# A decoder trunk in float32r: the low parts of its weights by an adding transfer, three-deep rings, squares in two tiles

## The chip, the cores and the metric

One core of a Trainium2 chip runs the whole program in one launch. The metric is the device time of one execution in microseconds (us). Two runs of the kernel before took 2085.44 and 2081.3 us, median 2083.37.

## What is computed

Two layers over x of shape (512 positions, 1024 channels), float32. Each layer has a feed-forward, a mixer and a second feed-forward:

```python
for l in range(DEPTH):                                   # DEPTH = 2
    x = x + 0.5 * _swiglu(_rms_norm(x, norm_ffn1[l]), ffn1_w_gate[l], ffn1_w_up[l], ffn1_w_down[l])
    h = _rms_norm(x, norm_mix[l])
    proj = (h @ w_in[l]).astype(jnp.float32)
    p_rwkv = _token_shift(proj[..., :D_SHIFT], shift_mu[l])
    y_rwkv = _rwkv7_mixer(p_rwkv, ...)                   # 6 heads of 64, a recurrence over time
    y_attn = _attention_mixer(proj[..., ...], ...)       # 6 heads of 64, three dilated windows
    y_conv = _conv_mixer(proj[..., ...], ...)            # 256 channels, 31 taps
    mix = jnp.concatenate([y_rwkv, y_attn, y_conv], axis=-1).astype(x.dtype)
    x = x + mix @ w_out[l]
    x = x + 0.5 * _swiglu(_rms_norm(x, norm_ffn2[l]), ffn2_w_gate[l], ffn2_w_up[l], ffn2_w_down[l])
```

`_swiglu` is `(silu(x @ w_gate) * (x @ w_up)) @ w_down` with 2816 hidden channels. All weights are float32 and come from DRAM.

## The kernel before, in words

x lies transposed in SBUF, channels on the 128 partitions, eight tiles x[j] of 128x512. Every large product is made in float32r from two parts of each factor, a high part (the value cast to float32r) and a low part (the value minus the high part): `mm3` (L116 to L121) issues three matmuls, high by high, high by low, low by high, into one PSUM tile.

**A weight slot.** `slot` (L105 to L114) brings in one piece of weights of up to 128x1024. SP issues the load into a tile `raw` (ring of three), ACT casts it into `hi` (L112), and DVE subtracts, lo = raw - hi (L113). `hi` and `lo` have rings of RB buffers each. There are 368 slots. A slot of 1024 columns feeds 24 matmuls of 512 columns.

**Feed-forward** (`ffn`, L224). For each of 22 hidden tiles f a gate slot and an up slot are multiplied with the norm's xh and xl. `gated` (L213) then makes g and u from PSUM with the norm's factor R on DVE (L216, L218), silu on ACT (L217), the product s*u on POOL (L219), the high part ah on ACT (L124) and the low part al on DVE (L125). After that each of eight output tiles j takes three slots of the down weights (8, 8 and 6 tiles of 128, L267). DVE adds the result to x[j] (L271), and `norm_tile` (L167) prepares the next norm: xh on ACT (L172), xl on DVE (L173), the square on ACT into the tile "sq" (L180, the first one into acc, L177), the running sum acc on POOL (L181). `norm_sum` (L195) reduces acc on PE, POOL takes the power (L186), `norm_spread` (L203) spreads it, and ACT copies it into R (L208).

**Mixer** (`mixer`, L290). 14 slots of the input projection `win` are worked through by `columns`; the preparation of the recurrence for three head pairs (`first`, `scores`, `fourth` and others) is woven in: GG (L491) and AR (L476) on DVE, XM (L498, L514) and BF (L508) on POOL. The 31 taps of the convolution (L1001, DVE) have a low priority and fill DVE. Then come 12 slots of the attention projections (`att_cols`, 768 columns each) beside the chunks of the recurrence (s1 to s4; p3 makes Z, L637; Sf, L665, on POOL), then attention, convolution and the output projection (`out`, 22 slots of 256 to 640 columns per layer). The mixer ends with eight slots of 384 columns, nine matmuls each, and after each the update of x[j] (L717) and `norm_tile`.

**Order.** A scheduler puts the instructions of each engine into a fixed order; each engine then works through its own queue in that order and waits at its head. A buffer of a ring is written again only when all readers of its former content are done. SP's queue holds the loads of weights, and among them the stores and loads of x and small transfers of the mixer.

Of the kernel before, what the change touches and what calls it, by code (L numbers as in the profile page):

```python
# [9 lines left out]
F32 = mybir.dt.float32  # L10
F32R = mybir.dt.float32r
AF = mybir.ActivationFunctionType
ALU = mybir.AluOpType
PSUM = bass.MemoryType.PSUM

P = 128
D = 1024
T = 512
# [1 line left out]
F = 2816  # L20
FT = F // P
EPS = 1e-6
RB = 2
LOWP = 3000
CPAD = 40
XPAD = 56
# [55 lines left out]
class Kern:  # L82
    def __init__(self, ctx, tc, I, out):
        self.tc, self.nc, self.I, self.out = tc, tc.nc, I, out
        self.depth = 2
        self.uid = 0
        self.ahead = []
        self.cp = ctx.enter_context(tc.tile_pool(name="cp", bufs=1))
        self.ring = ctx.enter_context(tc.tile_pool(name="ring", bufs=3))
        self.xpool = ctx.enter_context(tc.tile_pool(name="xpool", bufs=1))  # L90
        self.nrm = ctx.enter_context(tc.tile_pool(name="nrm", bufs=1))
        self.dp = ctx.enter_context(tc.tile_pool(name="dp", bufs=1, space=bass.MemoryType.DRAM))
        self.ps = ctx.enter_context(tc.tile_pool(name="ps", bufs=1, space=PSUM))
# [11 lines left out]
    def slot(self, src, cols, nm="w"):  # L105

        nc = self.nc
        raw = self.ring.tile([P, 1024], F32, tag="raw", name=self.n("raw"))
        hi = self.ring.tile([P, 1024], F32R, tag="hi", name=self.n("hi"), bufs=RB)
        lo = self.ring.tile([P, 1024], F32R, tag="lo", name=self.n("lo"), bufs=RB)  # L110
        self.wdma = nc.sync.dma_start(out=raw[:, :cols], in_=src)
        nc.scalar.copy(hi[:, :cols], raw[:, :cols])  # L112
        nc.vector.tensor_tensor(lo[:, :cols], raw[:, :cols], hi[:, :cols].bitcast(F32), op=ALU.subtract)  # L113
        return hi, lo  # L114

    def mm3(self, out, whi, wlo, xhi, xlo, first, last):  # L116
# [50 lines left out]
    def norm_tile(self, j):  # L167

        nc = self.nc
        x = self.x[j]  # L170
        g = self.gains[:, self.nidx * KT + j : self.nidx * KT + j + 1]
        nc.scalar.activation(self.xh[j], x, AF.Copy, scale=g)  # L172
        nc.vector.scalar_tensor_tensor(  # L173
            self.xl[j], x, g, self.xh[j].bitcast(F32), op0=ALU.mult, op1=ALU.subtract
        )
        if j == 0:
            nc.scalar.activation(self.acc, x, AF.Square)  # L177
        else:
            sq = self.nrm.tile([P, T], F32, tag="sq", name=self.n("sq"))
            nc.scalar.activation(sq, x, AF.Square)  # L180
            nc.gpsimd.tensor_tensor(self.acc, self.acc, sq, op=ALU.add)  # L181

# [949 lines left out]
```

## Time and profile before

| what | value |
| --- | --- |
| median of two runs | 2083.37 us |
| the profiled execution's own time | 2081.86 us |
| its span | 2080.1 us |
| granted clock of PE, mean | 0.99 |
| feed-forward stages | about 31 to 397, 698 to 1059 and 1059 to 1427, 1726 to 2080 us |
| mixers | about 397 to 698 and 1427 to 1726 us |
| HBM read | 183.47 MB |

The stages are read from the places where the sum of a norm is reduced in the chain of waits (L199 at 390.5, 698.6, 1059.5, 1420.4 and 1726.0 us). A row of a group of instructions reads: line, engine, operation, output<-input with partitions x elements, the count, then the busy time in us, the mean ns of one, and the idle time of the engine just before them with what ended it. A row of a wait reads: who, for whom, us in total, times, the longest. A row of a stage reads: its bounds and length, busy time and count of each engine, the granted clock, the DMA engines' share, GB/s.

### The profile page before, as it was taken

The numbers are of one execution on the slowest core, as the hardware profiler recorded it, in microseconds if no ns is written. First come the engines' busy times: TensorE is split into PE (matmuls) and PEld (weight loads), VectorE is DVE, ScalarE is ACT, GpSimd is POOL, SyncE is SP. The second block draws the span as 40 slices with busy tenths as digits, with TensorE's granted clock in tenths as the row PEclk, the third lists the DMA queues.
The fourth block names the chain that finished last, engine by engine and source line by source line (L and its number), as shares of the span: only waits on it lengthen the run. The fifth ranks groups of instructions, "written<-read, shape, count | busy, mean of one in ns | idle before, by whom it ended". The sixth has DMA issues, their size and how long they took to land.

```text
span 2080.1 us, 25896 instructions
## 1 busy us (share of the span) xinstructions
PE 2031.8 (98%) x10406; PEld 1653.1 (79%) x10406; DVE 1121.5 (54%) x1565; ACT 740.0 (36%) x1136; POOL 330.4 (16%) x298
## 2 busy tenths in 40 slices
PE   7999999999899999999999999999899999999999
PEld 5888888777776888888888888887687678888887
DVE  4555432598866654552345544336997665454422
ACT  4323222463365433222223232225533653232221
POOL 3111001131420311110111111012223211110000
PEclk9999999999999999999999999999999999999999
DMA  4333333312321433333333233332222133333332
GB/s 142 98 94 99 99 109 107 105 59 61 84 62 59 126 94 101 95 96 92 103 92 101 92 101 96 114 116 84 57 87 77 50 93 101 95 99 101 99 109 76
DMA packets 81863, 193.79 MB, mean 93 GB/s; under 512 B 26640, under 2 KB 32272, under 8 KB 81744
## 3 DMA queue, kind: packets, MB, share of 16 engines
q1 hardware_dynamic: 81312, 191.79, 30.1%
q8 instruction: 81, 1.33, 0.3%
q10 hardware_dynamic: 432, 0.36, 0.1%
q14 instruction: 38, 0.31, 0.0%
HBM read 183.47 MB, written 8.65 MB: 92 GB/s over the span
## 4 chain that ended last, share of the span: by engine, by line
PE 86%; DVE 8%; POOL 2%; issue 2%; ACT 2%; DMA 0%; SPq 0%; POOLq 0%; ACTq 0%; DVEq 0%
PE psg L119 25%; PE psg L121 25%; PE psg L120 25%; DVE lo L113 2%; DVE cacc L1001 1%; PE psg L915 1%; DVE Ei L584 1%; PE psb L485 1%; DVE tm L578 1%; PE psc L950 1%; PE psg L867 1%; POOL ast L895 1%; PE psg L941 1%; POOL acc L181 1%; PE psg L869 1%
## 5 line engine op out<-in xcount | busy, mean ns | idle before, releaser
L112 ACT CAST hi<-raw 128x1024 fp32r<-128x1024 f32 (+3 forms) x368 | 350.7, 953 | 1001.3 <-PE psg L120 575.4
L113 DVE TENSOR_TENSOR lo<-raw,hi 128x1024 fp32r<-128x1024 f32 (+3 forms) x368 | 508.2, 1381 | 347.1 <-ACT hi L112 321.1
L119 PE MATMUL psg<-xh,hi 128*128 128x512 f32 x1632 | 644.3, 395 | 7.1 <-ACT xh L172 7.1
L121 PE MATMUL psg<-xh,lo 128*128 128x512 f32 x1632 | 643.2, 394 | 1.2 <-DVE lo L113 1.1
L120 PE MATMUL psg<-xl,hi 128*128 128x512 f32 x1632 | 643.0, 394 | 0.0
L119 PEld LDWEIGHTS psg<-xh,hi 128*128 128x128 f32 x1632 | 309.5, 190 | 74.2 <-ACT xh L172 7.1
L121 PEld LDWEIGHTS psg<-xh,lo 128*128 128x128 f32 x1632 | 309.2, 189 | 67.9 <-DVE lo L113 2.7
L120 PEld LDWEIGHTS psg<-xl,hi 128*128 128x128 f32 x1632 | 309.2, 189 | 66.7 <-issue 2.9
L120 PE MATMUL psg<-al,hi 128*128 128x512 f32 x704 | 274.2, 389 | 0.0
L119 PE MATMUL psg<-ah,hi 128*128 128x512 f32 x704 | 274.2, 389 | 0.0
L121 PE MATMUL psg<-ah,lo 128*128 128x512 f32 x704 | 274.2, 389 | 0.0
L219 POOL TENSOR_TENSOR s<-s,u 128x512 f32<-128x512 f32 x88 | 113.6, 1291 | 808.7 <-ACT hi L112 652.2
L218 DVE TENSOR_TENSOR u<-psg,R 128x512 f32<-128x512 f32 x88 | 60.8, 691 | 272.0 <-PE psg L121 272.0
L121 PEld LDWEIGHTS psg<-ah,lo 128*128 128x128 f32 x704 | 132.2, 188 | 27.6
L119 PEld LDWEIGHTS psg<-ah,hi 128*128 128x128 f32 x704 | 132.2, 188 | 27.4
L120 PEld LDWEIGHTS psg<-al,hi 128*128 128x128 f32 x704 | 132.2, 188 | 27.1
L216 DVE TENSOR_TENSOR g<-psg,R 128x512 f32<-128x512 f32 x88 | 60.8, 691 | 132.6 <-PE psg L121 130.1
L181 POOL TENSOR_TENSOR acc<-acc,sq 128x512 f32<-128x512 f32 x42 | 68.4, 1628 | 379.8 <-ACT sq L180 379.8
L1001 DVE SCALAR_TENSOR_TENSOR cacc<-z,par,cacc 128x482 f32<-128x482 f32 (+14 forms) x120 | 95.2, 793 | 1.8
L124 ACT CAST ah<-s 128x512 fp32r<-128x512 f32 x88 | 54.9, 624 | 113.1 <-POOL s L219 113.1
L867 PE MATMUL psg<-hi,xh 128*128 128x384 f32 x192 | 68.7, 358 | 2.5 <-ACT nat L892 2.5
L868 PE MATMUL psg<-lo,xh 128*128 128x384 f32 x192 | 65.1, 339 | 0.0
(208 smaller groups left out, 1800.7 us busy)
## 6 DMA issues: line engine op xcount, KB each, us to landing
raw<-in_wgu_dram SPq DMA_DIRECT2D x176, 512.0 KB, 3.5
raw<-in_wd_dram SPq DMA_DIRECT2D x64, 512.0 KB, 3.5
raw<-in_win_dram SPq DMA_DIRECT2D x28, 512.0 KB, 3.5
raw<-in_wd_dram SPq DMA_DIRECT2D x32, 384.0 KB, 3.1
raw<-in_watt_dram SPq DMA_DIRECT2D x24, 384.0 KB, 3.1
raw<-in_wout_dram SPq DMA_DIRECT2D x28, 192.0 KB, 2.3
xs<-x SPq DMA_DIRECT2D x16, 256.0 KB, 2.0
x<-xs SPq DMA_DIRECT2D x16, 256.0 KB, 3.0
```

The source lines that it names most:

```text
L112: nc.scalar.copy(hi[:, :cols], raw[:, :cols])
L113: nc.vector.tensor_tensor(lo[:, :cols], raw[:, :cols], hi[:, :cols].bitcast(F32), op=ALU.subtract)
L119: mm(out, lhsT=whi, rhs=xhi, start=first, stop=False)
L120: mm(out, lhsT=whi, rhs=xlo, start=False, stop=False)
L121: mm(out, lhsT=wlo, rhs=xhi, start=False, stop=last)
L181: nc.gpsimd.tensor_tensor(self.acc, self.acc, sq, op=ALU.add)
L216: nc.vector.tensor_tensor(t[0], p[0], self.R, op=ALU.mult)
L218: nc.vector.tensor_tensor(t[1], p[1], self.R, op=ALU.mult)
L219: nc.gpsimd.tensor_tensor(t[2], t[2], t[1], op=ALU.mult)
L867: mm(o, lhsT=self.xh[kk][:, t], rhs=hi[:, s], start=kk == 0, stop=False)
L868: mm(o, lhsT=self.xh[kk][:, t], rhs=lo[:, s], start=False, stop=False)
L1001: nc.vector.scalar_tensor_tensor(a[:, d:], z[:, 0 : T - d], pa("dww", u * CW + j), a[:, d:], op0=ALU.mult, op1=ALU.add)
```

## The change

Four things. RB, the depth of the rings `hi` and `lo`, becomes 3. The first four slots are made as before. In all others ACT writes minus hi into lo, and a transfer issued by POOL adds raw, from SBUF to SBUF, into lo. The square of `norm_tile` goes by turns into the tiles "sq" and "R".

```diff
-RB = 2
+RB = 3
...
+        self.begun = 0
...
         nc.scalar.copy(hi[:, :cols], raw[:, :cols])
-        nc.vector.tensor_tensor(lo[:, :cols], raw[:, :cols], hi[:, :cols].bitcast(F32), op=ALU.subtract)
+        if self.begun < 4:
+            self.begun += 1
+            nc.vector.tensor_tensor(lo[:, :cols], raw[:, :cols], hi[:, :cols].bitcast(F32), op=ALU.subtract)
+        else:
+            nc.scalar.activation(lo[:, :cols], hi[:, :cols].bitcast(F32), AF.Copy, scale=-1.0)
+            nc.gpsimd.dma_start(out=lo[:, :cols], in_=raw[:, :cols], accum_op=ALU.add)
         return hi, lo
...
         if j == 0:
             nc.scalar.activation(self.acc, x, AF.Square)
         else:
-            sq = self.nrm.tile([P, T], F32, tag="sq", name=self.n("sq"))
+            sq = self.nrm.tile([P, T], F32, tag=("sq", "R")[j % 2], name=self.n("sq"))
             nc.scalar.activation(sq, x, AF.Square)
             nc.gpsimd.tensor_tensor(self.acc, self.acc, sq, op=ALU.add)
```

The load of `raw` waited in SP's queue for DVE's subtraction of three slots earlier; now it waits for the adding transfer of three slots earlier. Names below carry the scheduler's numbers; lines after the change are up to six higher.

POOL's queue where the first feed-forward begins, before: the last sum, the power, then nothing but products.

```order
L181 TENSOR_TENSOR acc_136<-acc_136,sq_172 128x512
L186 TENSOR_TENSOR rnt<-rnt,mh 128x4
L219 TENSOR_TENSOR s_314<-s_314,u_313 128x512
L219 TENSOR_TENSOR s_325<-s_325,u_324 128x512
L219 TENSOR_TENSOR s_398<-s_398,u_397 128x512
```

The same place now:

```order
L187 TENSOR_TENSOR acc_136<-acc_136,sq_172 128x512
L192 TENSOR_TENSOR rnt<-rnt,mh 128x4
L119 DMA lo_336<-raw_334 128x1024
L119 DMA lo_368<-raw_366 128x1024
L225 TENSOR_TENSOR s_314<-s_314,u_313 128x512
L225 TENSOR_TENSOR s_325<-s_325,u_324 128x512
L119 DMA lo_411<-raw_409 128x1024
L119 DMA lo_443<-raw_441 128x1024
L225 TENSOR_TENSOR s_400<-s_400,u_399 128x512
```

Two transfers stand ahead of each product s*u from here to the end of the stage.

ACT's queue in the middle of the first gate and up stage, before: one cast of a weight between silu and the cast of ah.

```order
L112 CAST hi_627<-raw_626 128x1024
L217 ACTIVATE s_617<-g_615 128x512
L112 CAST hi_658<-raw_657 128x1024
L124 CAST ah_622<-s_617 128x512
L112 CAST hi_700<-raw_699 128x1024
```

The same stage now:

```order
L113 CAST hi_1010<-raw_1009 128x1024
L118 ACTIVATE lo_1011<-hi_1010 128x1024
L130 CAST ah_930<-s_925 128x512
L113 CAST hi_1042<-raw_1041 128x1024
L223 ACTIVATE s_1000<-g_998 128x512
L118 ACTIVATE lo_1043<-hi_1042 128x1024
L113 CAST hi_1085<-raw_1084 128x1024
L118 ACTIVATE lo_1086<-hi_1085 128x1024
```

Each cast of a weight is followed by the write of minus hi (L118), directly or after a silu.

POOL's queue in the first mixer, beside the attention projections, before (ast and nat belong to the norm of attention's heads, Sf to the recurrence):

```order
L895 TENSOR_TENSOR ast_3747<-ast_3747,mh 128x6
L897 TENSOR_TENSOR nat_3749<-nat_3749,ast_3747 128x384
L665 TENSOR_TENSOR Sf_3958<-SVU_2572,fd_2577 64x192 x2
L665 TENSOR_TENSOR Sf_4144<-SVU_2572,fd_2577 64x192 x2
L895 TENSOR_TENSOR ast_3747<-ast_3747,mh 128x6
```

The same place now:

```order
L901 TENSOR_TENSOR ast_3830<-ast_3830,mh 128x6
L903 TENSOR_TENSOR nat_3832<-nat_3832,ast_3830 128x384
L119 DMA lo_3999<-raw_3997 128x768
L671 TENSOR_TENSOR Sf_4044<-SVU_2636,fd_2641 64x192 x2
L119 DMA lo_4087<-raw_4085 128x768
L119 DMA lo_4178<-raw_4176 128x768
L671 TENSOR_TENSOR Sf_4232<-SVU_2636,fd_2641 64x192 x2
L901 TENSOR_TENSOR ast_3830<-ast_3830,mh 128x6
```

Transfers stand between the results that the recurrence and the attention take from POOL.

## The prediction

> **What bounds the kernel now.** I read the page's busy shares first, then a table by stage, then the waits of PE, then the DMA rows.
>
> ```profile
> PE 2031.8 (98%) x10406; PEld 1653.1 (79%) x10406; DVE 1121.5 (54%) x1565; ACT 740.0 (36%) x1136; POOL 330.4 (16%) x298
> 80.00:240.00 160.00, 160.00 (x707) 132.52 (x707) 81.03 (x74) 48.33 (x59) 18.97 (x15) 1.00 0.31 98
> 397.00:500.00 103.00, 94.73 (x448) 71.86 (x447) 92.53 (x134) 59.06 (x91) 27.38 (x24) 0.92 0.19 56
> 500.00:560.00 60.00, 58.31 (x492) 51.55 (x492) 55.63 (x117) 23.02 (x42) 20.19 (x17) 1.00 0.34 90
> 560.00:640.00 80.00, 74.58 (x727) 55.19 (x725) 54.05 (x152) 44.50 (x116) 19.21 (x28) 0.98 0.20 58
> 640.00:697.00 57.00, 56.44 (x302) 42.30 (x302) 37.35 (x71) 29.46 (x59) 10.77 (x11) 1.00 0.35 103
> 1427.00:1530.00 103.00, 94.74 (x458) 71.94 (x457) 94.35 (x140) 59.29 (x91) 27.42 (x24) 0.95 0.20 56
> ```
>
> The columns of a stage are its length, the busy time of PE, PEld, DVE, ACT and POOL, the granted clock, the DMA share and GB/s. In the feed-forward (first stage shown) PE never stops: 707 matmuls in 160 us, 0.226 us each, so a weight slot of 24 matmuls lasts 5.43 us. DVE is half idle there, and work taken from it buys nothing. Only in the mixer (the other rows) is DVE nearly full (92.5 of 103 us) while PE has holes: 8.3, 1.7, 5.4 and 0.6 us, 15.9 us in all. The clock lost there is worth 8.2 us in the first mixer (0.08 of 103) and 5.2 us in the second. Two mixers hold at most 32 + 13 = 45 us. What PE waits for in the first one:
>
> ```profile
> PE psb L644 <- DVE Z L637: 4.1, 2, 3.7
> PE psb L485 <- DVE GG L491: 3.5, 1, 3.5
> PE psb L530 <- DVE vv L402: 2.2, 1, 2.2
> PE psb L485 <- DVE AR L476: 1.6, 1, 1.6
> ```
>
> GG, vv and AR (7.3 us) are results queued on a full DVE; Z is a step of the serial chunk chain and stays.
>
> **The subtractions that leave.** Of 368 subtractions 364 go. The rows that price them and what takes their place:
>
> ```profile
> 397.00:500.00 103.00, 14.24 (x10) 0.92 0.19 56
> L112 ACT CAST hi<-raw 128x1024 fp32r<-128x1024 f32 x268 | 281.9, 1052 | 818.0 <-PE psg L120 510.2 <-issue 302.5 <-PE psg L121 2.8
> L119 PE MATMUL psg<-xh,hi 128*128 128x512 f32 x1632 | 644.3, 395 | 7.1 <-ACT xh L172 7.1
> q1 hardware_dynamic: 81312, 191.79, 30.1%
> raw<-in_wgu_dram SPq DMA_DIRECT2D x176, 512.0 KB, 3.5
> L219 POOL TENSOR_TENSOR s<-s,u 128x512 f32<-128x512 f32 x88 | 113.6, 1291 | 808.7 <-ACT hi L112 652.2 <-DVE u L218 131.6 <-ACT s L217 24.9
> L218 DVE TENSOR_TENSOR u<-psg,R 128x512 f32<-128x512 f32 x88 | 60.8, 691 | 272.0 <-PE psg L121 272.0
> L124 ACT CAST ah<-s 128x512 fp32r<-128x512 f32 x88 | 54.9, 624 | 113.1 <-POOL s L219 113.1
> ```
>
> The first row is that stage for the line of the subtraction alone: 14.2 of DVE's 92.5 us. DVE falls to 78.3 of 103 and the taps, of low priority, can move into the room. I take two thirds of the 7.3 us: 4.9 us, and of the lost clock the share that the holes shrink by, 4.9 / 8.3 = 0.59: 4.8 us in the first mixer, 3.1 in the second. That is -9.7 and -8.0, **-17.7 us**; bounds 0 and -45.
>
> **The new chain of a slot in the feed-forward.** When PE leaves a slot, ACT casts the next hi (1.05 us), then writes minus hi (no row; same tile, same engine: 1.05), with a silu or a cast of 0.6 us between or behind; then POOL issues the transfer. Behind the waiting transfer stand the products s*u (1.29 us), which only ah and al need, a slot pair later. From PE's release to the issue I count 2.7 us. With three buffers the low part must land before PE has used the two others and come back: 3 x 5.43 - 5.43 - 2.7 = **8.2 us** for issue to landing. In the down stage slots average 22 matmuls, 4.98 us: 3 x 4.98 - 4.98 - 2.5 = 7.5 us for 0.92 of the bytes.
>
> The transfer itself has no row: nothing here adds in a transfer or starts one from POOL. By the DMA row a plain 512 KB needs 1.71 us of all 16 engines (30.1% of 2080.1 us is 626 us for 191.79 MB) and lands after 3.5 us, so 1.8 us are latency. Low end: it behaves like a plain load, 3.5 us. High end: three passes at the load's pace (two reads and the write one after the other) 5.1 us, plus 1.8, plus a whole load in the way 1.7, plus an issue as long as POOL's product, 1.3: 9.9 us. I take two passes, as the adding reads two operands where a load reads one and writes go beside reads: 1.8 + 3.4 + 1.3 + half a load 0.9 = 7.4 us, nearer the upper end but below 8.2. It is then hidden behind PE's two slots at 0 us; if that cover is gone, each slot costs a third of the excess. In the down stage 0.92 of the transfer parts gives 7.0 against 7.5.
>
> [...]
>
> Engine time per slot would be 1.71 + 3.42 = 5.13 us of 5.43: it fits, with 6% to spare. The loads move too: raw is freed now by the landed transfer, not by DVE. At the latest that is as PE starts the slot, 5.4 us before the next hi is cast from it, against 3.5 us to land; what waits behind such a load in SP's queue in the feed-forward is only the next load and a store of x.
>
> **Costs in the mixer.** The casts of the first stage, and what PE waits for ACT:
>
> ```profile
> 397.00:500.00 103.00, 11.00 (x11) 0.92 0.19 56
> PE psg L867 <- ACT nat L892: 1.2, 2, 0.8
> PE psc L950 <- ACT pT L942: 0.7, 1, 0.7
> PE psb L436 <- ACT tmp L433: 0.5, 1, 0.5
> ```
>
> ACT gets as many copies again, 59 + 11 = 70 of 103 us. PE's waits on it are small today (2.4 us); I take +1.5 us per mixer; bounds 0 and 8. POOL's transfers stand ahead of small results (ast, Sf, gst) that DVE then waits for: +2 us; bounds 0 and 25. The end of the mixer goes from slot to slot of 9 matmuls:
>
> ```profile
> 676.48 0.69 DVE x L717
> 677.17 0.97 DVE lo L113
> 678.35 0.50 ACT L112 CAST hi<-raw 128x384 fp32r<-128x384 f32 x1
> 678.73 0.68 DVE x L717
> 679.40 0.97 DVE lo L113
> raw<-in_wout_dram SPq DMA_DIRECT2D x28, 192.0 KB, 2.3
> ```
>
> A slot takes 2.23 us (677.17 to 679.40), PE's own part 2.04. The ring now gives (2.04 + 1.3 for two copies of 0.5 and their gap + 3.9 for the transfer) / 3 = 2.41, where 3.9 is the plain 2.3 plus a second pass of 0.6 and an issue of 1.0. That is +0.18 x 8 = +1.4 us; bounds 0 and 7. Together +4.9 us per mixer, **+9.8 us**.
>
> **Squares in two tiles.** At the start the sums on POOL form the chain:
>
> ```profile
> 12.81 1.62 POOL acc L181
> 15.17 1.63 POOL acc L181
> 17.53 1.63 POOL acc L181
> PE psc L199 <- POOL acc L181: 3.8, 1, 3.8
> ```
>
> They come every 2.36 us though one takes 1.63, because the next square waits for the tile. Seven without that gap end about 4 us earlier, and PE's one wait of 3.8 us goes to about 0.2: **-3.6 us**; bounds 0 and -3.8. Elsewhere PE does not wait for that sum.
>
> **Sum.** -17.7 + 9.8 - 3.6 = -11.5 us on the profiled execution's 2081.86 us (span 2080.1 and 1.8 around it): 2070.4. The two runs shown have their median 1.5 us above it, so I forecast 2072 us.
>
> **Rivals.**
>
> 1. Slower: the ring is too shallow for the landing time. It decides from 8.2 us of issue to landing on, in gate and up. For it: 7.4 is close, DMA engines would be 94% taken, and there is no row. Against: loads now run only 30% of the time and come one at a time. At the high end of 9.9 us a gate or up slot takes (5.43 + 2.7 + 9.9) / 3 = 6.01 us, +0.58 on 176 slots, 102 us; a down slot (4.98 + 2.5 + 9.1) / 3 = 5.53, +0.55 on 96, 53 us. That is 2072 + 155 = 2227 us.
>
> 2. Slower: DMA engines become the bound. It decides when the adding takes over 5.43 - 1.71 = 3.7 us of all engines, 2.2 passes. Three passes, 5.13 + 1.71 = 6.84 us a slot, cost 1.41 x 176 + (6.27 - 4.98) x 96 = 372 us: 2444 us. Against: a load's 1.71 us includes the way from DRAM, which the adding does not have.
>
> 3. Slower: POOL's in-order queue in the mixers. The 26 weights of the two input projections (14 and 12) have a transfer ahead of a product or power that the chunk chain or attention waits for; at one issue of 1.3 us each on the path, 34 us per mixer instead of 2: 2072 + 64 = 2136. Against: POOL is busy 27 of 103 us there.
>
> [...]
>
> 5. Faster by over 2%: all of the mixers' holes and lost clock go and the costs stay at half: 2083 - 45 - 3.6 + 5 = 2040. Against: Z and the attention's waits are not DVE's queue.
>
> 6. The third buffer is idle, because raw stays at three and is held longer: this is a way into rival 1, not a time of its own.
>
> **How the numbers follow.** Forecast 0.54; rival 1 0.15; rival 2 0.13; rival 3 0.08; rival 4 0.04; rival 5 0.06. The range runs from 2045 (inside rival 5) to 2260 (all of rival 1, some of rival 2), with about 0.14 outside. The forecast's own range is 2050 to 2110. Over or under 2%, about 42 us, is what a measurement of this kernel can tell from no change: faster 0.07 (rival 5 and a little of the forecast), same 0.56 (forecast, rival 4), slower 0.37 (rivals 1, 2, 3).
>
> **What would show it.** Right: in the feed-forward still 0.226 us per matmul and no wait of PE for lo; the DMA share near 0.9 there; issue to landing of the adding transfer 6 to 8 us; DVE near 78 of the mixer's first 103 us, and the wait for GG gone; PE's wait for the first sum gone. Wrong: PE waiting for lo in every slot (rival 1 if the DMA engines have gaps, rival 2 if they have none), or PE's mixer waits naming POOL or ACT (rival 3).

## The result and the profile after

The changed kernel takes 2104.08 us (median of 2103.39 and 2104.77), the kernel before 2083.37: ratio 1.0099, 95% interval 1.0083 to 1.0116. It is 1% slower; the forecast was 0.5% faster, 2072 us, and the time lies inside the range. The profiled execution has a span of 2101.6 us, 21.5 more than before.

First the stages. PE spreads the norm's sum once per feed-forward or mixer, always at the same place of the program, so the starts of these matmuls mark the stages. Of before (start and length in us):

```profile
396.76 1.05 PE L191 MATMUL psc<-tab,rnt 128*128 128x128 f32 x8
704.78 1.05 PE L191 MATMUL psc<-tab,rnt 128*128 128x128 f32 x8
1426.62 1.05 PE L191 MATMUL psc<-tab,rnt 128*128 128x128 f32 x8
1732.22 1.05 PE L191 MATMUL psc<-tab,rnt 128*128 128x128 f32 x8
```

And of after:

```profile
390.16 1.05 PE L197 MATMUL psc<-tab,rnt 128*128 128x128 f32 x8
710.91 1.05 PE L197 MATMUL psc<-tab,rnt 128*128 128x128 f32 x8
1433.29 1.05 PE L197 MATMUL psc<-tab,rnt 128*128 128x128 f32 x8
1752.39 1.05 PE L197 MATMUL psc<-tab,rnt 128*128 128x128 f32 x8
```

The first feed-forward ends 6.6 us earlier. The first mixer lasts 320.7 us instead of 308.0, the second 319.1 instead of 305.6: 26 us lost there. What is left, about 2 us, is in the later feed-forwards.

Next the busy shares of after and its table by stage:

```profile
PE 2040.1 (97%) x10406; PEld 1656.5 (79%) x10406; DVE 645.1 (31%) x1201; ACT 1075.4 (51%) x1500; POOL 620.9 (30%) x662
```

```profile
80.00:240.00 160.00, 160.00 (x707) 132.51 (x706) 30.45 (x44) 77.92 (x89) 44.98 (x45) 1.00 0.86 193
390.00:493.00 103.00, 92.54 (x447) 70.08 (x446) 81.57 (x123) 68.64 (x100) 32.12 (x34) 0.93 0.47 110
```

In the feed-forward PE does the same 707 matmuls in 160 us without a gap. In the mixer's first stage, whose row is set 7 us earlier as the mixer begins so much earlier, DVE has fallen from 92.5 to 81.6 of 103 us, and yet PE's busy time is 92.5 us, 2.2 less than the 94.7 before. DVE was relieved and PE got nothing. The waits of PE in the first mixer, up to where its attention projections begin:

```profile
PE psb L442 <- ACT tmp L439: 3.8, 2, 3.2
PE psb L491 <- DVE AR L482: 2.6, 1, 2.6
PE psb L491 <- DVE GG L497: 2.6, 2, 2.2
PE psb L536 <- DVE vv L408: 1.2, 1, 1.2
```

GG, vv and AR are together at 6.4 us for 7.3 before; that for ACT's tmp, 0.5 before, is now 3.8 and the largest. What ACT itself waited for there is shown under "What the relief of DVE is worth". The adding transfer, which had no row before, by the page of the profile (the queue of software transfers; its issues and the copy on ACT; two rows of time from issue to landing):

```profile
q0 software_dynamic: 52416, 168.84, 43.9%
L119 POOL DMA_DIRECT2D lo<-raw x364 | 317.2, 878 | 1033.3 <-ACT lo L118 981.6
L118 ACT ACTIVATE lo<-hi 128x1024 fp32r<-128x1024 f32 (+4 forms) x364 | 348.3, 957 | 8.1
lo<-raw POOLq DMA_DIRECT2D x264, 512.0 KB, 5.7
raw<-in_wgu_dram SPq DMA_DIRECT2D x176, 512.0 KB, 4.8
```

512 KB land after 5.7 us; loads beside it take 4.8 us where they took 3.5. Last, the end of the first mixer. Before, in the 20 us that end 10.8 us ahead of the spread:

```profile
674.00:694.00 20.00, 19.44 (x84) 15.30 (x83) 17.48 (x22) 13.83 (x23) 10.07 (x7) 1.00 0.63 185
```

Now, the same place in stretches of five microseconds:

```profile
680.00:685.00 5.00, 2.66 (x12) 1.87 (x10) 1.61 (x3) 1.93 (x3) 0.99 (x1) 1.00 0.77 218
685.00:690.00 5.00, 2.99 (x9) 1.90 (x9) 2.93 (x4) 4.02 (x7) 3.78 (x4) 0.69 0.66 170
690.00:695.00 5.00, 3.71 (x13) 3.32 (x14) 0.28 (x2) 3.35 (x4) 2.80 (x3) 0.50 0.54 149
695.00:700.00 5.00, 5.00 (x19) 4.02 (x18) 0.00 (x0) 0.00 (x0) 1.26 (x2) 0.79 0.87 172
```

PE stands still for 5.6 of 20 us, where it stood for 0.6 before, and the granted clock falls to 0.50 behind it: worth at most 0.31 + 0.50 + 0.21 of five us each, 5.1 us more, and 3.8 if only the time in which PE was busy is counted. The chain that holds PE there, from the timeline:

```profile
678.27 0.50 PE L127 MATMUL psg<-mix,lo 128*128 128x512 f32 x1 [1.37 <-DMA lo<-raw]
678.27 21.57 SPq L112 DMA_DIRECT2D raw<-in_wgu_dram  x5
678.76 0.88 POOL L119 DMA_DIRECT2D lo<-raw  x1
683.07 1.04 ACT L113 CAST hi<-raw 128x1024 fp32r<-128x1024 f32 x1 [3.53 <-DMA raw<-in_wgu_dram]
685.42 0.50 PE L127 MATMUL psg<-mix,lo 128*128 128x512 f32 x1 [2.76 <-DMA lo<-raw]
```

The low part of the last small slot, issued at 678.76, is there only at 685.42, 6.7 us later, where 192 KB have a median of 3.2 us in this kernel; loads of 512 KB run beside it, five of them issued from 678.27 on; that they are the reason is the author's guess, which no run tests. And the first load of the feed-forward is issued at 678.27; ACT waits 3.53 us for it with the norm's xh and squares queued behind.

### The profile page after: what moved, and what is told of

The parts are those of the page before. It is cut to its first block, busy times and chain, and to the rows that moved or that the text cites. A ratio compares the mean times of both kernels' runs of the same rounds, so it can differ in the third digit from the quotient of the medians.

```text
span 2101.6 us, 27007 instructions
## 1 busy us (share of the span) xinstructions
PE 2040.1 (97%) x10406; PEld 1656.5 (79%) x10406; DVE 645.1 (31%) x1201; ACT 1075.4 (51%) x1500; POOL 620.9 (30%) x662
## 3 DMA queue, kind: packets, MB, share of 16 engines
q0 software_dynamic: 52416, 168.84, 43.9%
## 4 chain that ended last, share of the span: by engine, by line
PE 84%; DVE 6%; ACT 4%; DMA 3%; POOL 2%; issue 1%; SPq 0%; ACTq 0%; POOLq 0%; DVEq 0%
PE psg L125 25%; PE psg L126 24%; PE psg L127 24%; DMA lo<-raw 2%; DVE Ei L590 1%; DVE tm L584 1%; ACT hi L113 1%; PE psb L491 1%; PE psg L921 1%; PE psg L873 1%; DMA raw<-in_wgu_dram 1%; PE psc L956 1%; PE psg L875 1%; PE psg L874 1%; PE psg L947 1%
## 5 line engine op out<-in xcount | busy, mean ns | idle before, releaser
L119 POOL DMA_DIRECT2D lo<-raw x364 | 317.2, 878 | 1033.3 <-ACT lo L118 981.6
L118 ACT ACTIVATE lo<-hi 128x1024 fp32r<-128x1024 f32 (+4 forms) x364 | 348.3, 957 | 8.1
L277 DVE SCALAR_TENSOR_TENSOR x<-psg,x 128x512 f32<-128x512 f32 x32 | 22.1, 692 | 400.8 <-PE psg L127 400.8
L131 DVE TENSOR_TENSOR al<-s,ah 128x512 fp32r<-128x512 f32 x88 | 60.9, 693 | 185.9 <-ACT ah L130 185.9
```

The source lines that it names most:

```text
L118: nc.scalar.activation(lo[:, :cols], hi[:, :cols].bitcast(F32), AF.Copy, scale=-1.0)
L119: nc.gpsimd.dma_start(out=lo[:, :cols], in_=raw[:, :cols], accum_op=ALU.add)
L131: self.nc.vector.tensor_tensor(lo, src, hi.bitcast(F32), op=ALU.subtract)
```

## The experiments

All times are medians on the chip against the kernel before on the same chip (2083.0 to 2084.0 us). Single executions of one kernel spread by about 3 us up and down, a few by 5 to 9, so profiles are read here for waits, and differences for medians and intervals.

### Which part costs: four edits of the change

Three theories stood at first. H: the loss is where the mixers end, because raw is held until the transfer has landed, and loads wait. O: it is there, because the new order has PE wait for the next norm's sum too early. P: it is spread over the mixers' stages. In all edits `src.tensor.name` names the weight that a slot loads.

The sum of the next norm held behind FFN2's first two slots on PE (the change's order has it 45 matmuls earlier):

```diff
-                        self.norm_sum()
+                        with self.tc.issue_after(self.lastmm.ins):
+                            self.norm_sum()
```

> The changed kernel, with the reduction of a norm's sum on PE tied behind the last matmul of the slot it follows in the program; in the changed kernel it had come out 45 matmuls earlier after each mixer. Two theories for the 21 us: H, the raw buffers stay taken until the adding transfer has landed, so that at the mixer's end the next load, its cast and what stands behind it on ACT come late; O, the scheduler's other order on PE makes PE wait for POOL's sum there and lets the clock fall. O expects the loss of each handover to go, 2104 - 20 = 2084 us. H expects only the wait for the sum itself to go, 3 to 4 us each: 2097 us, with PE still waiting for lo at the mixer's end.

2102.11 us, ratio 1.0078 (1.0050 to 1.0105). The place of that sum on PE is not the cause of more than a few us.

A fourth raw buffer, so that a load is not held by a transfer:

```diff
-        raw = self.ring.tile([P, 1024], F32, tag="raw", name=self.n("raw"))
+        raw = self.ring.tile([P, 1024], F32, tag="raw", name=self.n("raw"), bufs=4)
```

> The changed kernel with four raw buffers in place of three. H expects most of the handover's loss to go though every transfer stays: 2086 us, and no wait of PE for lo at the mixer's end. If instead ACT's doubled copies there are the cause, the time stays at 2104 us.

2102.83 us, 1.0089 (1.0067 to 1.0111). The load comes earlier and nothing is won; PE then waits 8.1 us for landings between 670 and 715 us. That the held raw buffer is the cause falls.

The output projection's slots by DVE, as before the change:

```diff
-        if self.begun < 4:
+        if self.begun < 4 or src.tensor.name == "in_wout_dram":
```

> The changed kernel, with the low parts of the 44 output-projection slots made by DVE again; all other slots by the adding transfer. H expects raw to be free early at the mixer's end and 10 us to come back per mixer: 2084 us. A third theory, P (the mixer's loss is spread, from POOL's and ACT's queues in its first stages), expects no more than 5 us back: 2099 us.

2091.74 us, 1.0035 (1.0022 to 1.0048), half way between H and P: 12 of the 21 us come from the output projection's slots at the end of the mixers, the rest from elsewhere.

No adding at all (rings of three and two square tiles stay):

```diff
-        if self.begun < 4:
+        if True:
```

> No adding transfer at all: the kernel before with rings of three and squares in two tiles. The first norm ended 6.6 us earlier in the changed kernel. If the squares and the third buffer did that, this kernel takes 2083 - 6 = 2077 us; if it needed a freed DVE, 2083 us.

2080.75 us, 0.9985 (0.9976 to 0.9994). The two small parts of the change are a slight gain together; the adding alone costs 23 us.

### The two small parts apart

The kernel before with one line changed each, `RB = 3`, or the squares' tag `("sq", "R")[j % 2]`.

> The kernel before with rings of three and nothing else (no adding transfer, one square tile). The kernel with rings of three and two square tiles, without the adding, had its start 3 us and its first feed-forward 4 us shorter, and its mixers 4 and 6.6 us longer in the profiled execution. Theory R (the deeper ring lengthens the mixers, since the fixed order puts low parts of the next weights ahead on DVE; the start is the squares'): mixers 308 to 312 us each, start as before but for PE's wait of 1.5 us for the spread of the norm, whose matmuls stand 24 later in this order; about 2086 us, 2084 to 2091. Theory S (the second square tile lengthens the mixers, the ring gives the start): 2077 to 2081 us.

> The kernel before with squares in two tiles and nothing else. PE, DVE, POOL and SP have the order of the kernel before; on ACT the squares move. Theory R: the mixers stay at 308 and 306 us; PE's wait of 3.8 us for the first sum goes, and with it the clock of 0.64 and 0.67 in the ten us behind it, which is worth 3.5 us; the wait of 1.5 us for the spread stays: 2076 to 2080 us, below both kernels so far. Theory S: the start gains nothing beyond 3 us, and the mixers are 2 to 6 us longer: 2083 to 2090 us.

The ring alone: 2086.31 us, 1.0013 (1.0004 to 1.0022), slower. The squares alone: 2077.07 us, 0.9964 (0.9952 to 0.9976). Theory R holds. The squares' gain is larger than PE's wait, as this table of the same ten microseconds shows (before, then with two square tiles):

```profile
25.00:35.00 10.00, 8.32 (x33) 6.73 (x34) 4.03 (x6) 2.56 (x4) 3.41 (x3) 0.66 0.33 107
```

```profile
25.00:35.00 10.00, 9.55 (x46) 8.06 (x47) 4.55 (x6) 3.42 (x5) 1.68 (x2) 1.00 0.34 110
```

Behind the wait of 3.8 us the clock was 0.66 for ten microseconds, 2.8 us more lost if the 8.3 us in which PE was busy are counted, at most 3.4. How the ring costs is seen in the waits of the kernel without adding, between 640 and 712 us:

```profile
PE psg L125 <- DVE xl L178: 2.3, 2, 1.9
```

Before, PE did not wait for xl there: with a third buffer the order puts three instead of two low parts of the next feed-forward (1.2 to 2.3 us each on DVE) ahead of the norm's last xl. That the whole 2.5 us come from this is argued, not shown: in the profile of the ring alone PE has the same wait, 2.5 us, and yet that mixer lasts 308.3 us as before.

### The end of the mixers: copy or landing

ACT writes minus high in the output projection's slots, and DVE does the adding:

```diff
-        if self.begun < 4:
+        if src.tensor.name == "in_wout_dram":
+            nc.scalar.activation(lo[:, :cols], hi[:, :cols].bitcast(F32), AF.Copy, scale=-1.0)
+            nc.vector.tensor_tensor(lo[:, :cols], raw[:, :cols], lo[:, :cols].bitcast(F32), op=ALU.add)
+        elif self.begun < 4:
```

> The change, but in the slots of the output projection DVE adds raw to minus hi where the transfer did; ACT writes minus hi there as in the change. Theory C (the second copy on ACT is what lengthens the end of the mixers): 2100 to 2105 us, as the change. Theory L (the time from POOL's issue to the landing of the transfer is): 2088 to 2094 us, as with those slots made wholly by DVE, 2091.7 us.

2095.81 us, 1.0051 (1.0038 to 1.0063), between the two, nearer to L. The transfers' landing is the larger part; the copy's 0.0016 has an interval that reaches to zero.

### Is the third buffer used

The change with `RB = 2`.

> The change with rings of two instead of three. By the prediction's sum for a ring, with the landing time that the change's profile shows: a gate or up slot (5.43 + 2.7 + 5.7) / 2 = 6.9 us, +1.5 on 176 slots; a down slot (4.98 + 2.5 + 5.2) / 2 = 6.3 us, +1.4 on 96 slots: 390 us, and some in the mixers: 2500 us, 2400 to 2550. If the third buffer is idle (the sixth rival): 2104 us.

2434.53 us, 1.1681 (1.1661 to 1.1701). Its feed-forward in the table by stage, and its row of landing times:

```profile
80.00:240.00 160.00, 143.13 (x599) 110.25 (x599) 26.29 (x38) 66.13 (x76) 37.07 (x37) 1.00 0.68 164
```

```profile
lo<-raw POOLq DMA_DIRECT2D x264, 512.0 KB, 4.8
```

A slot takes 24 x 160 / 599 = 6.41 us. The prediction's ring sum with this kernel's own landing time gives (5.43 + 2.7 + 4.8) / 2 = 6.47. The expected 2500 us were too many since the landing falls from 5.7 to 4.8 us; the DMA share there is 0.68 instead of 0.86. The sum for a ring stands, and the third buffer is needed.

### What the relief of DVE is worth

A ladder on one base: adding in the feed-forward alone (the mixers' slots by DVE); then without low parts in the two input projections (the high part stands in their place, PE has the same matmuls); then with ACT's copies there and no adding; the kernel with the transfers too is the one with the output projection by DVE, above. And once with no low parts in the output projection either.

```diff
+        if src.tensor.name in ("in_win_dram", "in_watt_dram"):
+            return hi, hi
-        if self.begun < 4:
+        if self.begun < 4 or src.tensor.name in ("in_wout_dram", "in_win_dram", "in_watt_dram"):
```

> The change, with the adding transfer in the feed-forward alone: all slots of the mixers have their low parts by DVE's subtraction. Theory F (the feed-forward hides the adding, as its profile shows): as the kernel with rings of three and two square tiles but no adding, 2080.8 us; 2079 to 2084. Theory H2 (the slots of the second feed-forward that are made while the mixer ends cost what is lost): 2087 to 2092 us, near the kernel in which only the output projection was by DVE, 2091.7 us.

> As the kernel with the adding in the feed-forward alone, but the low parts of the weights of the two projections (win, watt) are left out: the high part is used in their place, PE has the same matmuls, and nothing subtracts, copies or transfers for them. It shows what the relief of DVE is worth with no price. Theory V (the relief is there, as the prediction had it, and the copies on ACT or the transfers eat it): 17.7 us below the kernel with the adding in the feed-forward alone, 2063 us; at least 10 below. Theory N (there is no relief: DVE's results come late by the chain, not by the queue): within 4 us of it, 2077 to 2084 us.

> As the one before, but ACT writes minus high into the low tile in the slots of the two projections and nothing adds: the low parts are wrong by the missing addition, and DVE is relieved as there. It shows what ACT's copies cost without transfers. Theory V with ACT as the eater: 2080 to 2085 us, at least 10 above the one before; with the transfers as the eater: 2063 to 2068 us, and the 2091.7 us of the kernel that has the transfers too comes from those. Theory N: 2082 to 2088 us.

> The low parts of the output projection's weights are left out too, the high part in their place: the mixers have no work for low parts at all. By the ends of the mixers, where DVE's last results (x and xl behind the low parts of the next weights) hold the first sum of the feed-forward: theory V 2055 us, theory N 2070 to 2078 us, 4 to 8 below the kernel that leaves out those of the two projections alone.

In that order: 2085.36 us, 1.0007 (0.9997 to 1.0017); 2079.81, 0.9983 (0.9975 to 0.9992); 2085.34, 1.0005 (0.9995 to 1.0015); 2081.38, 0.9985 (0.9977 to 0.9994). So the relief without any price is worth about 5 us of the forecast 17.7, the kernel with ACT's copies has lost it again, and the transfers cost some 6 more. Theory V falls, and N, with "within 4 us", is close. Leaving out the output projection's low parts too gives nothing (N had expected 4 to 8). The expectation F for the first of the four, 2079 to 2084, was missed by little: at the start of each second feed-forward PE waits 3.2 us for a landing there too.

Why the relief is worth so little, the kernel without those low parts shows. DVE is busy 85.2 of 103 us in the first stage (391 to 494 us; the taps have moved into part of the room), and PE still waits 4.8 us for GG. On DVE and POOL just ahead of that GG:

```profile
453.92 1.77 DVE L484 TENSOR_TENSOR AR<-r,Pm 128x512 f32<-128x512 f32 x1
455.62 1.75 DVE L1009 SCALAR_TENSOR_TENSOR cacc<-z,par,cacc 128x507 f32<-128x507 f32 x1
456.79 4.67 POOL L516 TENSOR_TENSOR BF<-BK,fd 64x1024 f32<-64x1024 f32 x2
457.30 2.40 DVE L512 SCALAR_TENSOR_TENSOR r<-r,par,kn 128x512 f32<-128x512 f32 x1
459.62 3.17 DVE L1009 SCALAR_TENSOR_TENSOR cacc<-z,par,cacc 128x508 f32<-128x508 f32 x2
462.81 0.69 DVE L499 TENSOR_TENSOR GG<-psb,tab 64x512 f32<-64x512 f32 x1
```

The trace of before had it too, at its wait of 3.5 us:

```profile
462.13 0.69 DVE L399 TENSOR_TENSOR sraw<-psg,R 128x512 f32<-128x512 f32 x1
463.17 5.20 POOL L508 TENSOR_TENSOR BF<-BK,fd 64x1024 f32<-64x1024 f32 x2
464.21 2.39 DVE L504 SCALAR_TENSOR_TENSOR r<-r,par,kn 128x512 f32<-128x512 f32 x1
466.53 2.39 DVE L402 SCALAR_TENSOR_TENSOR vv<-sraw,der,st 128x512 f32<-128x512 f32 x1
469.70 0.49 PE L485 MATMUL psb<-AR,BK 64*128 64x128 f32 x2 [3.46 <-DVE GG L491]
```

r and vv take 0.74 us elsewhere and 2.39 us each while POOL makes BF: 2 x 1.65 = 3.3 us of the 3.46 that PE waits. sraw, which reads one tile in PSUM, keeps its 0.69 us beside POOL's mask of XM (L514, until 463.2). So it is not the length of DVE's queue that makes GG late, but POOL's products: beside them these instructions of DVE, which read two tiles in SBUF, take 2.39 us against 0.74. The trace of after has both kinds beside BF itself: AR, with two inputs in SBUF, takes 2.39 us at 457.32 and 0.68 without BF; sraw keeps 0.69 us at 476.51.

The trace of before has the hold the other way round too, once. At 416.26 us DVE's k began 0.17 us ahead of a BF: k, kn and a subtraction behind it kept 0.75, 0.68 and 1.22 us, and that BF took 4.08 us where the shortest took 2.04. And it was there to be seen in the feed-forward, where it costs nothing: of the 268 subtractions of 1024 columns the 82 beside a product s*u took 2.33 us each, the 145 beside nothing of POOL 1.23.

The wait for ACT's tmp in the changed kernel, the largest there, has the same origin:

```profile
412.44 2.06 POOL L514 TENSOR_TENSOR BF<-BK,fd 64x1024 f32<-64x1024 f32 x1
412.65 2.39 DVE L408 SCALAR_TENSOR_TENSOR k<-sraw,der,st 128x512 f32<-128x512 f32 x1
415.08 0.72 ACT L439 ACTIVATE tmp<-k,par 128x512 f32<-128x512 f32 x1 [3.01 <-DVE k L408]
```

ACT stands idle for 3.0 us until k is there, and k is held beside BF, 2.39 us for 0.75. PE's wait of 3.2 us is put down to ACT, the last link, but it is not ACT's copies that fill that time. In the third kernel of the ladder, with ACT's copies and nothing added in the projections, ACT waits as long for k (3.01 us), there behind a tap that takes 2.37 us beside BF. So the 4.6 us between the second and the third kernel are what the copies cost together with the order that they bring; that ACT's own time is the price is not shown.

### BF away from POOL

The twelve products BF by DVE (`V.tensor_tensor` for `G.tensor_tensor`), on the kernel with two square tiles and nothing else of the change; the same on the kernel without the projections' low parts; BF as a scaled copy on ACT, which leaves out the factor fd; BF and the masks of XM by DVE.

> The kernel before with squares in two tiles (2077.1 us), and the twelve products BF of the mixers made by DVE instead of POOL. Theory B (POOL's products hold DVE's instructions with two inputs from SBUF for as long as they run, and that is what makes GG and vv late): those instructions take 0.74 us throughout, PE's waits for GG and vv (11.8 us) fall by half or more; 2066 to 2073 us. Theory Q (what counts is how much stands in DVE's queue; the twelve products add some 14 us to it): 2078 to 2085 us.

> The kernel that leaves out the low parts of the two projections' weights (2079.8 us; the high part in their place), with BF by DVE. Theory B: the relief can now be used, 2066 to 2073 us. Theory Q: 2080 to 2084 us.

> The kernel before with squares in two tiles (2077.1 us), with BF as a plain scaled copy on ACT: the factor fd is left out, and POOL and DVE have no work for BF. Theory B: 2063 to 2071 us, somewhat below the kernel with BF on DVE. Theory Q: 2074 to 2079 us, as DVE's queue is no shorter than in the kernel with squares in two tiles.

> As the kernel with BF by DVE, and the twelve products of XM with the mask by DVE too, so that POOL has no large product in the first stage of the mixers. Theory B: AR, which took 1.1 us instead of 0.69 beside them, is freed as well, but each product now stands in DVE's queue: 2064 to 2073 us. Theory Q: 2083 to 2092 us.

In that order: 2052.58 us, 0.9852 (0.9838 to 0.9865); 2062.0, 0.9897 (0.9881 to 0.9912); 2065.26, 0.9910 (0.9895 to 0.9926); 2057.71, 0.9878 (0.9865 to 0.9892). All four gain, theory Q falls, and three of the four gain more than theory B had. Moving the masks as well costs 5 us over BF alone. Of the first one, the mixer's first stage (the row set to where this mixer begins, 393 us), two of PE's waits over the whole span, and the group of r:

```profile
393.00:496.00 103.00, 100.24 (x513) 78.48 (x513) 96.84 (x153) 62.67 (x94) 12.24 (x18) 0.98 0.22 64
```

```profile
PE psb L485 <- DVE GG L491: 2.4, 4, 0.9
PE psb L644 <- DVE Z L637: 0.4, 2, 0.2
```

```profile
L504 DVE SCALAR_TENSOR_TENSOR r<-r,par,kn 128x512 f32<-128x512 f32 x6 | 4.4, 738 | 0.0
```

DVE is fuller than before (96.8 us for 92.5) and PE gets 100.2 of 103 us instead of 94.7. r is back at 0.738 us. GG, 7.4 us in both mixers with the squares alone, is 2.4. The gain, 24.5 us, is more than theory B had (to 2066): PE's wait for Z also goes, from 8.3 to 0.4 us. With BF on ACT that wait stays (8.9 us) and the gain is 11.8 us, within B's range. By this about half of the 24.5 is the hold at GG, vv and AR; that is an estimate, as each of the four kernels is also a new order of the queues, and why Z comes in time in the one order and not in the other is left open.

Without the low parts of the projections nothing more comes: 2062.0 us is the first one's 2052.6 plus what the ring (4) and the adding in the feed-forward (5) had cost. If those two prices are the same on this base, which no run shows, DVE's relief is worth nothing even with the hold gone.

Two last ones: the change with BF by DVE, and the kernel before with BF by DVE.

> The change with the twelve products BF by DVE. If DVE's relief can be used once the hold is gone and pays for the adding: 2050 to 2060 us, at or below the 2052.6 us of the squares with BF by DVE. If the price of the adding in the mixers stays (the copies on ACT and the transfers' landing, 23 us over the same kernel without the adding): 2074 to 2084 us.

> The kernel before with BF by DVE and nothing else. If the two gains add (squares 6.7, BF 24.5): 2059 us, 2056 to 2062. If the gain of BF hung on the squares: above 2065 us.

2082.27 us, 0.9996 (0.9985 to 1.0007): the price of the adding in the mixers stays. But the change too gains 21.8 us by it, and PE's wait for ACT's tmp (L439), 7.5 us over the whole span in the change, falls to 1.6. And 2056.17 us, 0.9865 (0.9849 to 0.9881): the gain of BF stands alone. The fastest version is the one with two square tiles and BF by DVE, 2052.6 us, 1.5% below the kernel before.

## Why the prediction was wrong

The ratios of the experiments times 2083.5 us give a ledger; each step is good to about 3 us, the last two to 4 or 5:

| step | from, to | us |
| --- | --- | --- |
| squares in two tiles | 1, 0.9964 | -7.5 |
| rings of three on top | 0.9964, 0.9985 | +4.4 |
| adding in the feed-forward | 0.9985, 1.0007 | +4.6 |
| DVE relieved of the projections' low parts | 1.0007, 0.9983 | -5.0 |
| ACT's copies there | 0.9983, 1.0005 | +4.6 |
| transfers there | 1.0005, 1.0035 | +6.3 |
| copies in the output projection | 1.0035, 1.0051 | +3.3 |
| transfers there | 1.0051, 1.0099 | +10.0 |
| sum | | +20.7 |

Against the sum of -11.5 the ledger is 32.2 us higher: 12.7 of it is the relief and 15.1 the end of the mixers with the feed-forward's first slots. Either of these two steps alone takes the forecast gain away. That 2104 us lies inside the range is no support for the sum, whose sign was wrong.

Point by point:

- **The relief, -17.7: wrong, and the first of the two steps that failed.** It read "results queued on a full DVE" from a busy share and the name DVE in the waits. The busy share of DVE fell nearly as worked out (81.6 us for 78.3), but the waits were those of single results behind instructions of DVE that POOL's products held to three times their length (2.39 us for 0.74); the trace of before showed it in the rows of r and vv. Measured without any price: -5.0. The prediction also set Z aside as a step of the chain that stays; with BF by DVE that wait fell from 8.3 to 0.4 us.
- **The end of the mixers, +1.4 each: wrong in its cover, and the second step that failed.** The term took a steady ring of small slots. That part is right: from 667.11 to 678.76 us POOL issues every 2.33 us, where 2.41 was worked out. Left out was the step from slots of 2 us to the first of the feed-forward: a load of 4.8, cast and copy of 1.04 each, and 5.7 us from POOL's issue to the landing stand in line, 12.6 us by these rows, against 3.5 + 1.04 + 1.2 = 5.7 before; and the last small transfer lands late (6.7 us for 3.2). Three small slots cover 6 us of it. Measured +13 for both mixers with the output projection, and 4.6 more for the feed-forward's own slots, which the prediction had at 0.
- **ACT +1.5 and POOL +2 per mixer**: together 7 us forecast and 10.9 measured for the projections. The size is near, the mechanism is not shown: PE's largest wait in the first stage now names ACT, but ACT stands there for DVE's k, held beside BF.
- **The third buffer, 0**: +4.4 on top of the squares, +2.5 alone. The prediction gave the order that a deeper ring makes no price.
- **The start, -3.6**: right cause, too small, since the clock behind the wait was left out; -7.5 by ratio. In the profiles the first feed-forward ends 6.6 us earlier in the change.
- **The feed-forward's steady part**: right. Landing 5.7 us for an estimated 7.4, under the 8.2 that the ring allows; engine time 43.9% of 2101.6 us for 168.84 MB, 2.87 us per 512 KB for 3.42; DMA share 0.86 for 0.94; no wait. The two passes, with writes beside reads, were an assumption that no run shows; measured is 2.87 us against a load's 1.71, a factor of 1.68.
- **The rivals**: 1 and 2 did not come. 3 had the mixers as the place, and its 2136 us were too many: an issue took 0.87 us, not 1.3, which makes its sum 2113. How much of the transfers' 6.3 us in the projections is POOL's queue and how much is landing was not told apart; in the changed kernel PE waits 2.7 us for landings at the attention projections (L874) and 0.2 us for a result of POOL there (nat). For rival 4's chance of 0.04 no run shows a ground: POOL's 364 issues take 0.85 to 1.24 us, median 0.87, with DVE as busy as it is. The hold that this kernel has is between POOL's products and DVE.

## What to carry to other kernels

Before an engine is relieved, look at the rows of the instruction that is waited for and of those just ahead of it, and follow an idle engine that a wait names to what it waits for itself: if one of these rows lasts longer than its like elsewhere (here 2.39 us for 0.74), what makes it long is the thing to move, and the engine's busy share says nothing about it. The change lengthens a slot's chain (load, cast, copy, issue, landing); in the steady part of the feed-forward the depth of the ring hid that here (707 matmuls in 160 us, as before), and it was paid at each place where small slots give way to large ones (13 us for both mixers). A new buffer is also a new order (here +2.5 us), and has to be timed alone.

## What the runs showed of the hardware

- A DVE instruction of 128x512 with two inputs in SBUF took 2.39 us instead of 0.74 beside POOL's 64x1024 product; with one input in PSUM it kept 0.69, beside that product and beside POOL's mask. A 128x1024 subtraction took 2.33 us instead of 1.23 beside POOL's product s*u.
- A DVE instruction that began 0.17 us ahead of POOL's product kept its 0.75 us, and the product took 4.08 us instead of 2.04.
- Beside POOL's issue of a transfer, 0.87 us, a product AR took 0.68 us, as alone, and each of 84 subtractions al 0.69.
- An adding transfer of 512 KB inside SBUF took 2.87 us of all 16 engines, where a plain load takes 1.71.
- At the end of the mixer PE stood for 2.3 us of one stretch of five and for 2.0 of the next; the clock was 0.69 in that second one and 0.50 in the third.
